# Hybrid decoder layer, one core: the state-space input, q and k projections change which operand stands still in TensorE

## The chip, the cores and the metric

The kernel runs on one core of one Trainium2 chip. The metric is the device time of one execution in microseconds (us); lower is better.

## The reference, cut to what matters

```
h    = rmsnorm(x, ln_g)                      # x: 256 tokens x 4096, float32
proj = h @ w_in                              # 4096 x 12288
p_x, p_gate, q, k, v, a_gate, s_u, s_gate = split(proj)    # 1024 1024 2048 2048 2048 2048 1024 1024
y_pool = pool_mixer(p_x); y_attn = stick_breaking_attention(q, k, v)   # 16 heads of 128
y_ssm  = s5_mixer(s_u)                       # scan over tokens, GELU, GLU with w_glu 1024 x 2048
y = concat(rmsnorm(y_i, g_i) * silu(gate_i)) # pool, attention, state space
out = rmsnorm(x + y @ w_out, final_g)        # w_out 4096 x 4096
```

All is float32. On TensorE each float32 operand is split into a rounded part `hi` and a remainder `lo` (both of the type fp32r), and a product is three matmuls: hi·hi, hi·lo and lo·hi.

## The kernel before, in words

**The stream.** The weights come in 528 pieces of 512 KB (two blocks of 128 rows x 512 columns; "sub" below), in an order that is written out in `IN_ORDER` (L40). 512 columns of one weight make a **unit**: 16 subs for a unit of `w_in` or `w_out`, 4 for one of `w_glu`. The order is su, su (state-space input), px, px, pg, pg, sg, sg, then v, q, k three times, four units of `w_glu`, v, q, k once more, four of ag, and eight of `w_out`. The loop at L860 takes one sub after the other: it issues the loads (SP queue, four subs ahead, L871), splits the weights of the sub two ahead (`split`, L210: ACT rounds `hi` at L228, DVE subtracts `lo` at L231, which the profile shows as its helper L82), and issues the matmuls of this sub into the unit's PSUM tile `pm` (two buffers of 128 x 2 x 512). At the end of a unit `finish` (L766) evacuates the tile. Generators then carry the branches' own work: `pump(side_q, 3)` (L916) takes three steps per sub from the queue of pooling, gates and attention, L917 to L921 take steps of the state-space scan. The framework's scheduler orders the instructions of each engine from a simulated time line and from their dependencies; only SP's order is by hand.

**Two kinds of units.** The normalised and split input `xhl` lies with channels on the partitions: for each of 32 channel blocks, hi and lo of 256 tokens.

- `mm_tok` (L234; px, pg, sg, v, glu, ag, out): 128 tokens stand in the array, 512 weight columns move. A sub is 12 matmuls of 512 columns, a unit of 16 subs is 192. The product has tokens on the partitions; `scaled` (L657) evacuates it with two ACT instructions that multiply by the norm's factor `rtok`, one number per partition.
- `mm_chan` (L241; su, q, k): 128 weight columns stand, 256 tokens move. A sub is 24 matmuls of 256 columns, a unit is 384. The product has channels on the partitions, which is what the scan and the attention's scores want; `chan_scaled` (L663) evacuates it with two DVE instructions that multiply by `rrow`, the norm's factors along the free axis. `norm_x` (L269) makes `rrow` from `rtok` with two matmuls against the identity (L277) and a copy (L278).

There are 10 units of the second kind: 2 su, 4 q, 4 k. The first su unit's product waits in its PSUM tile until the norm is known, at sub 12 of the second unit (L866). 64 PE transposes against the identity exist elsewhere: `transposed` (L291, L296) turns the gated branch outputs, four blocks of 128 x 128 into one PSUM tile `ps_t`, evacuated by ACT. The pool of PSUM tiles tagged `ps` has two buffers and serves these, the scan (`ps_bu`, `ps_y`) and attention (`ps_av`).

**Waits around the change.** `uT` (the turned su product) is read by DMAs that the ACT queue issues (L531, `side_dma`) and by DVE (L577). The tiles `qt` and `kt` are read by the score matmuls of attention (L598, L599), which run in the next unit.

Of the kernel before, what the change touches and what calls it, by code (L numbers as in the profile page):

```python
# [19 lines left out]
P = 128  # L20
# [35 lines left out]
def body(tc, a, out, ctx):  # L56
# [41 lines left out]
    oneneg = cp.tile([P, P], F32R, name="oneneg")  # L98
    identb = cp.tile([P, P], BF16, name="identb")
    maskb = cp.tile([P, P], BF16, name="maskb")  # L100
    ones = cp.tile([P, P], F32, name="ones")
    prm = cp.tile([P, 72], F32, name="prm")
    rtok = cp.tile([P, 2], F32, name="rtok")
    rrow = cp.tile([P, L], F32, name="rrow")
    ln_g = prm[:, 0:32]
    branch_g = prm[:, 32:64]
    d_skip = prm[:, 64:72]
# [10 lines left out]
        stt(t, t, -0.5, dst, ALU.mult, ALU.mult)  # L118
        stt(dst, t, 1.5, dst, ALU.add, ALU.mult)

# [1 line left out]
    wtiles, htiles = {}, {}  # L122
    held = []

# [113 lines left out]
            T.matmul(ps[t], stat[:, slot, 0, sl], lo, start=False, stop=False)  # L238
            T.matmul(ps[t], stat[:, slot, 1, sl], hi, start=False, stop=last)  # L239

    def mm_chan(ps, slot, hi, lo, first, last):  # L241
        for j in range(4):
            o = ps[:, j // 2, (j % 2) * L:(j % 2) * L + L]
            c = slice(j * P, j * P + P)
            T.matmul(o, hi[:, c], xhl[:, slot, 0, :], start=first and j % 2 == 0, stop=False, skip_group_check=True)  # L245
            T.matmul(o, hi[:, c], xhl[:, slot, 1, :], start=False, stop=False, skip_group_check=True)  # L246
            T.matmul(o, lo[:, c], xhl[:, slot, 0, :], start=False, stop=last, skip_group_check=True)  # L247

# [1 line left out]
    state = {}  # L250
    xtiles = {}
    x_sums = cp.tile([P, 2, 8], F32, name="x_sums")
# [16 lines left out]
    def norm_x():  # L269
        s = cp.tile([P, 2], F32, name="s_x", tag="s_b", bufs=2)  # L270
        V.tensor_reduce(s, x_sums, mybir.AxisListType.X, ALU.add)
        rsqrt_mean(rtok, s, 2, D, cp, "rs")
        ps2 = pk.tile([P, 512], F32, tag="ps", bufs=2, name="ps_r")
        for t in range(2):
            rb = cp.tile([P, P], F32, tag="rb", bufs=1, name="rb")
            ts(rb, ones, rtok[:, t:t + 1], ALU.mult)
            T.matmul(ps2[:, t * P:t * P + P], rb, ident, start=t == 0, stop=True, skip_group_check=True)  # L277
        V.tensor_copy(rrow, ps2[:, 0:L])  # L278

# [1 line left out]
    def log1pexp_parts(z, l):  # L281
        act(l, z, AF.Abs)
        act(l, l, AF.Exp, scale=-1.0)
# [43 lines left out]
        if g2 is not None:  # L327
            tt(y, y, g2, ALU.mult)

# [1 line left out]
    pool_sums = cp.tile([P, 2, 2], F32, name="pool_sums")  # L331
    ypool = {}

# [39 lines left out]
        y = ypool.pop(u)  # L373
        yield from transposed(y, [4 * u + c for c in range(4)], keep(lambda kt: ypT[:, kt, :]))

# [1 line left out]
    uT = bp.tile([P, 8, L], F32, tag="k8", bufs=3, name="uT")  # L377
    glu = {}

# [202 lines left out]
            tt(uT[:, ct, :], y, l, ALU.mult)  # L582
            yield

# [1 line left out]
    aout = {}  # L586
    att_sums = cp.tile([P, 2, 4], F32, name="att_sums")

# [62 lines left out]
        else:  # L651
            yield from transposed(y, kts, direct)

# [1 line left out]
    cur = {}  # L655

    def scaled(ps, name):  # L657
# [2 lines left out]
            act(z[:, t, :], ps[:, t, :], AF.Copy, scale=rtok[:, t:t + 1])  # L660
        return z

    def chan_scaled(dst, ps, scale=None):  # L663
        row = rrow.unsqueeze(1).broadcast_to([P, 2, L])
        for h in range(2):
            src = ps[:, h, :].rearrange("p (c m) -> p c m", c=2)
            if scale is None:
                tt(dst[:, 2 * h:2 * h + 2, :], src, row, ALU.mult)
            else:
                stt(dst[:, 2 * h:2 * h + 2, :], src, scale, row, ALU.mult, ALU.mult)  # L670

    ssm_q, side_q = deque(), deque()

# [11 lines left out]
    def drain(q):  # L685
        pump(q, 1 << 30)

# [1 line left out]
    units = []  # L689
    for kind, c in IN_ORDER:  # L690
        units.append((kind, c, 8 if kind == "glu" else KT))
# [24 lines left out]

    def constants():
        nc.sync.dma_start(ident, a["cst"][0])
        V.memset(ones, 1.0)
        for i, dst in ((1, tneg), (2, oneneg), (3, maskb)):  # L720
            raw = cp.tile([P, P], F32, name="raw", tag="rb", bufs=1)
            nc.sync.dma_start(raw, a["cst"][i])
            act(dst, raw, AF.Copy)
        V.tensor_copy(identb, ident)
# [41 lines left out]
    def finish(kind, c, n, ps):  # L766
        nonlocal sgate
        if kind == "su":
            if n == 0:
                state["ps0"] = ps  # L770
                return
            chan_scaled(uT[:, 4:8, :], ps)
            u_done[0] = 8
        elif kind == "px":
            side_q.append(pool_unit(n, scaled(ps, "px")))
        elif kind == "pg":
            side_q.append(pool_gate(n, scaled(ps, "pgz")))
        elif kind == "sg":
            if n == 0:
                sgate = bp.tile([P, 2, 2 * NU], F32, tag="k8", bufs=3, name="sgate")  # L780
            z = scaled(ps, "sgz")

            def sgate_gen(z=z, n=n):
                sg = bp.tile([P, 2, NU], F32, tag="k4", bufs=6, name="sgm")
                sigmoid_of(z, sg)
                yield
                tt(sgate[:, :, n * NU:n * NU + NU], z, sg, ALU.mult)
                yield
            side_q.append(sgate_gen())
        elif kind == "v":  # L790
            cur["v"] = scaled(ps, "vt")
        elif kind in ("q", "k"):
            t = bp.tile([P, 4, L], F32, tag="k4", bufs=6, name=kind + "t")
            chan_scaled(t, ps, QS if kind == "q" else None)
            cur[kind] = t
            if kind == "k":
                if apool is None:
                    start_att()
                if n == 2:
                    start_late()  # L800
                side_q.append(attention(apool if n < 2 else lp, n, cur["v"], cur["q"], cur["k"]))
        elif kind == "glu":
            bias = lp.tile([P, NU], F32, tag="bias", bufs=1, name="bias")
            side_dma(bias, a["bgl"][n:n + 1, :].partition_broadcast(P))
            y = bp.tile([P, 2, NU], F32, tag="k4", bufs=6, name="gl")
            tt(y, ps, bias.unsqueeze(1).broadcast_to([P, 2, NU]), ALU.add)
            if n % 2 == 0:
                def gate_gen(y=y):
                    sg = bp.tile([P, 2, NU], F32, tag="k4", bufs=6, name="gs")
                    glu["sg"] = sg  # L810
                    sigmoid_of(y, sg)
                    yield
                side_q.append(gate_gen())
            else:
                def val_gen(y=y, n=n):
                    tt(y, y, glu.pop("sg"), ALU.mult)
                    yield
                    square_sums(glu_sums, y, n // 2)
                    yield
                    glu[n // 2] = y  # L820
                    if n == 3:
                        r = branch_norm(glu_sums, 1024)
                        ysT = bp.tile([P, 8, L], F32, tag="k8", bufs=3, name="ysT")
                        state["ysT"] = ysT
                        for u in range(2):
                            yu = glu.pop(u)
                            gated(yu, r, sgate[:, :, u * NU:u * NU + NU])
                            yield
                            yield from transposed(yu, [24 + 4 * u + c for c in range(4)], keep(lambda kt: ysT[:, kt - 24, :]))
                side_q.append(val_gen())  # L830
        elif kind == "ag":
            z = scaled(ps, "agz")
            if n == 2:
                drain(side_q)
                att_ctx.close()
                qp = ctx.enter_context(tc.tile_pool(name="rows", bufs=1, reuse_waits="tile"))
                side_q.append(sums_of_rows(qp, y_src))
            side_q.append(att_gate(lp, n, z))
            if n == 3:
                for i in range(28):  # L840
                    hi_lo(xhl[:, i, 0, :], xhl[:, i, 1, :], y_src(i))
        elif kind == "out":
            xr, fg = state["rest"]
            o = state["o"][:, :, n * NU:n * NU + NU]
            tt(o, ps, xr, ALU.add)
            for t in range(2):
                act(xr[:, t, :], o[:, t, :], AF.Square, accum_out=out_sums[:, t, n:n + 1])
            tt(o, o, fg.unsqueeze(1).broadcast_to([P, 2, NU]), ALU.mult)
# [11 lines left out]
    for i, (ui, s) in enumerate(subs):  # L860
# [5 lines left out]
        if ui == 1 and s == 12:  # L866
            with tc.high_priority():
                norm_x()
                chan_scaled(uT[:, 0:4, :], state.pop("ps0"))
            u_done[0] = 4  # L870
        while loaded < min(len(subs), i + 1 + LOAD_AHEAD):  # L871
            if loaded == 0:
                load_first()
# [23 lines left out]
        else:  # L897
            for kk in range(2):
                hi, lo = htiles.pop((i, kk))
                slot = 2 * s + kk  # L900
                first, last = slot == 0, slot == nk - 1
                if kind in ("su", "q", "k"):
                    mm_chan(ps, slot, hi, lo, first, last)
                else:
                    late = i >= N_SUB - HELD
                    mm_tok(psl, hhl if kind == "glu" else xhl, slot, hi, lo, first, last, (0,) if late else (0, 1))
                    if late:
                        delayed.append((slot, hi, lo, last))
        if s == nk // 2 - 1:
            n = nth.get(kind, 0)  # L910
            nth[kind] = n + 1
# [129 lines left out]
```

## Time and profile before

| | us |
|---|---|
| median of 3 runs | 1558.77 (1558.5 to 1559.57) |
| profiled execution, first to last instruction | 1556.4 |
| TensorE busy in it | 1538.2 |

The page of the profile gives the profiled execution's span; what lies around the span is taken as the 2.4 us by which the median stands above it. PE stands for TensorE's matmuls and PEld for its weight loads, DVE for VectorE, ACT for ScalarE, SP for SyncE. A matmul's own duration overlaps with its neighbours', so the cost of one in a dense stretch is the distance between starts.

### The profile page before, as it was taken

The page shows a single profiled execution, that of the slowest core. Times are in us where ns is not written, and L with a number is a line of the kernel's source. Part 1 is how long each engine was busy: PE and PEld are TensorE (multiplying, and loading weights), DVE is VectorE, ACT ScalarE, POOL GpSimd, SP SyncE. Part 2 cuts the span into 40 slices and gives each one's busy share as a digit, 9 for nine tenths or more (in the row PEclk, how much of TensorE's full clock was granted, in tenths as well). Part 3 has the DMA queues.
Part 4 walks back from the last instruction along what each step waited for, and adds up shares of the span by engine and source line. Part 5 has one row for each costly group of instructions (what it writes and reads, how often), then busy time and mean ns, then how long its engine had stood idle before and what let it go on. Part 6 is the DMA issues. An engine that isn't in the chain of part 4 may idle for free.

```text
span 1556.4 us, 25428 instructions
## 1 busy us (share of the span) xinstructions
PE 1538.2 (99%) x9164; PEld 1360.9 (87%) x9164; DVE 1201.6 (77%) x2325; ACT 913.9 (59%) x1637; POOL 0.2 (0%) x4
## 2 busy tenths in 40 slices
PE   8999999999999999999999999999999999999996
PEld 8998788888799989998998889988888888888885
DVE  7579978999898879897556745455678888888886
ACT  7655556666565555565546754456667655555554
POOL 0000000000000000000000000000000000000000
PEclk9999999999999999999999999999999999999999
DMA  8866656566655546554555555545556666666665
GB/s 320 306 214 205 195 162 205 186 206 194 205 188 185 187 156 197 176 175 162 183 186 180 180 185 183 183 159 186 190 178 193 212 220 220 216 214 210 204 222 198
DMA packets 94079, 308.45 MB, mean 198 GB/s; under 512 B 11777, under 2 KB 17665, under 8 KB 93953
## 3 DMA queue, kind: packets, MB, share of 16 engines
q1 hardware_dynamic: 84096, 296.08, 58.2%
q10 hardware_dynamic: 9856, 10.76, 2.3%
q8 instruction: 71, 1.16, 0.3%
q14 instruction: 56, 0.45, 0.1%
HBM read 299.45 MB, written 4.19 MB: 195 GB/s over the span
## 4 chain that ended last, share of the span: by engine, by line
PE 96%; DVE 2%; DMA 1%; ACT 1%; issue 0%; SPq 0%; DVEq 0%; ACTq 0%
PE pm L238 18%; PE pm L237 18%; PE pm L239 18%; PE pm L245 10%; PE pm L247 10%; PE pm L246 10%; PE ps L185 3%; PE pm L185 3%; DVE lo L82 1%; PE ps_y L572 1%; DMA w<-in_ws 1%; PE ps_bu L545 0%; ACT hi L228 0%; PE ps_z L598 0%; PE ps_p L356 0%; PE ps_t L296 0%
## 5 line engine op out<-in xcount | busy, mean ns | idle before, releaser
L82 DVE TENSOR_TENSOR lo<-w,hi 128x512 fp32r<-128x512 f32 (+1 forms) x1048 | 696.9, 678 | 273.1 <-ACT hi L228 266.0
L228 ACT ACTIVATE hi<-w 128x512 fp32r<-128x512 f32 x968 | 604.6, 629 | 503.2 <-PE pm L239 204.4
L238 PE MATMUL pm<-lo,xhl 128*128 128x512 f32 x1232 | 482.4, 392 | 0.0
L239 PE MATMUL pm<-hi,xhl 128*128 128x512 f32 x1232 | 480.8, 390 | 0.0
L237 PE MATMUL pm<-hi,xhl 128*128 128x512 f32 x1232 | 480.6, 390 | 0.0
L245 PE MATMUL pm<-xhl,hi 128*128 128x256 f32 x1280 | 363.8, 284 | 5.3 <-ACT xhl L94 5.3
L246 PE MATMUL pm<-xhl,hi 128*128 128x256 f32 x1280 | 363.5, 284 | 0.0
L247 PE MATMUL pm<-xhl,lo 128*128 128x256 f32 x1280 | 363.4, 284 | 0.0
L238 PEld LDWEIGHTS pm<-lo,xhl 128*128 128x128 f32 x1232 | 231.5, 188 | 48.9 <-issue 2.1
L239 PEld LDWEIGHTS pm<-hi,xhl 128*128 128x128 f32 x1232 | 231.4, 188 | 47.3 <-issue 1.2
L237 PEld LDWEIGHTS pm<-hi,xhl 128*128 128x128 f32 x1232 | 231.5, 188 | 46.9 <-issue 0.4
L245 PEld LDWEIGHTS pm<-xhl,hi 128*128 128x128 f32 x1280 | 246.6, 193 | 7.1 <-ACT xhl L94 5.3
L247 PEld LDWEIGHTS pm<-xhl,lo 128*128 128x128 f32 x1280 | 246.6, 193 | 1.2 <-issue 0.8
L246 PEld LDWEIGHTS pm<-xhl,hi 128*128 128x128 f32 x1280 | 246.6, 193 | 0.8 <-issue 0.4
L91 DVE SCALAR_TENSOR_TENSOR et<-et,pw,tr 128x16 f32<-128x16 f32 (+3 forms) x256 | 55.6, 275 | 2.3 <-ACT tr L94 1.9
L94 ACT ACTIVATE sums<-t 128x1024 fp32r<-128x1024 f32 x40 | 42.3, 1058 | 23.8 <-DVE t L82 23.3
L82 DVE TENSOR_TENSOR sums<-t,sums 128x1024 fp32r<-128x1024 f32 x40 | 48.9, 1223 | 8.8 <-ACT sums L94 8.7
L94 ACT ACTIVATE hi<-w 128x256 fp32r<-128x256 f32 x80 | 40.0, 518 | 22.4 <-PE pm L239 18.9
L185 PE MATMUL ps<-sums,s 128*128 128x256 f32 x240 | 46.5, 283 | 1.1 <-DVE sums L82 1.1
L94 ACT ACTIVATE tr<-et,pw 128x32 f32<-128x32 f32 (+3 forms) x128 | 44.7, 384 | 4.7 <-DVE et L91 2.0
L82 DVE TENSOR_TENSOR t<-w 128x512 f32<-128x512 f32 x40 | 27.6, 690 | 24.3 <-DMA w<-in_ws 24.0
L560 DVE TENSOR_TENSOR_SCAN tb<-rho,ta 128x256 f32<-128x256 f32 x64 | 40.6, 676 | 0.1
(258 smaller groups left out, 1261.3 us busy)
## 6 DMA issues: line engine op xcount, KB each, us to landing
w<-in_ws SPq DMA_DIRECT2D x527, 512.0 KB, 3.5
xsq<-in_xr SPq DMA_DIRECT2D x8, 512.0 KB, 7.2
xr<-in_xr SPq DMA_DIRECT2D x8, 512.0 KB, 4.5
out<-o SPq DMA_DIRECT2D x8, 512.0 KB, 4.0
xt<-in_xT SPq DMA_DIRECT2D x15, 256.0 KB, 6.1
b<-in_bst ACTq DMA_DIRECT2D x16, 192.0 KB, 3.6
u<-uT ACTq DMA_DIRECT2D x96, 32.0 KB, 3.0
fg<-in_fg SPq DMA_DIRECT2D x8, 256.0 KB, 5.9
```

Source lines behind the costliest of these rows:

```text
L82: V.tensor_tensor(o, x, y, op)
L91: V.scalar_tensor_tensor(o, x, s, y, op0, op1)
L94: S.activation(o, x, f, **kw)
L185: T.matmul(o, stat[:, p, :], mov[q], start=begin and k == 0, stop=end and k == 2, skip_group_check=True)
L228: made = S.activation(hi, w[:, kk, :], AF.Copy)
L237: T.matmul(ps[t], stat[:, slot, 0, sl], hi, start=first, stop=False)
L238: T.matmul(ps[t], stat[:, slot, 0, sl], lo, start=False, stop=False)
L239: T.matmul(ps[t], stat[:, slot, 1, sl], hi, start=False, stop=last)
L245: T.matmul(o, hi[:, c], xhl[:, slot, 0, :], start=first and j % 2 == 0, stop=False, skip_group_check=True)
L246: T.matmul(o, hi[:, c], xhl[:, slot, 1, :], start=False, stop=False, skip_group_check=True)
L247: T.matmul(o, lo[:, c], xhl[:, slot, 0, :], start=False, stop=last, skip_group_check=True)
L560: V.tensor_tensor_scan(tb[:, c, :], rho[:, pr:pr + 1].broadcast_to([P, L]), ta[:, c, :], 0.0, ALU.mult, ALU.add)
```

## The change

`mm_chan` and `chan_scaled` go; su, q and k units run through `mm_tok` and are evacuated by `scaled`, and a new generator `channels` turns the result with eight PE transposes in two groups of four, each evacuated by ACT into the tile that DVE wrote before. `rrow`, `ones` and the matmuls that made `rrow` go as well.

```diff
-    ones = cp.tile([P, P], F32, name="ones")
-    rrow = cp.tile([P, L], F32, name="rrow")
...
-    def mm_chan(ps, slot, hi, lo, first, last):
-        for j in range(4):
-            o = ps[:, j // 2, (j % 2) * L:(j % 2) * L + L]
-            c = slice(j * P, j * P + P)
-            T.matmul(o, hi[:, c], xhl[:, slot, 0, :], start=first and j % 2 == 0, stop=False, skip_group_check=True)
-            T.matmul(o, hi[:, c], xhl[:, slot, 1, :], start=False, stop=False, skip_group_check=True)
-            T.matmul(o, lo[:, c], xhl[:, slot, 0, :], start=False, stop=last, skip_group_check=True)
...
         rsqrt_mean(rtok, s, 2, D, cp, "rs")
-        ps2 = pk.tile([P, 512], F32, tag="ps", bufs=2, name="ps_r")
-        for t in range(2):
-            rb = cp.tile([P, P], F32, tag="rb", bufs=1, name="rb")
-            ts(rb, ones, rtok[:, t:t + 1], ALU.mult)
-            T.matmul(ps2[:, t * P:t * P + P], rb, ident, start=t == 0, stop=True, skip_group_check=True)
-        V.tensor_copy(rrow, ps2[:, 0:L])
...
-    def chan_scaled(dst, ps, scale=None):
-        row = rrow.unsqueeze(1).broadcast_to([P, 2, L])
+    def channels(z, dst, scale=1.0):
         for h in range(2):
-            src = ps[:, h, :].rearrange("p (c m) -> p c m", c=2)
-            if scale is None:
-                tt(dst[:, 2 * h:2 * h + 2, :], src, row, ALU.mult)
-            else:
-                stt(dst[:, 2 * h:2 * h + 2, :], src, scale, row, ALU.mult, ALU.mult)
+            ps = pk.tile([P, 512], F32, tag="ps", bufs=2, name="ps_c")
+            for c in range(2):
+                for t in range(2):
+                    T.transpose(ps[:, (c * 2 + t) * P:(c * 2 + t + 1) * P], z[:, t, (h * 2 + c) * P:(h * 2 + c + 1) * P], ident)
+            act(dst[:, 2 * h:2 * h + 2, :], ps.rearrange("p (c m) -> p c m", c=2), AF.Copy, scale=scale)
+            yield
+
+    def take_u(ps, n):
+        def gen(z=scaled(ps, "suz")):
+            yield from channels(z, uT[:, 4 * n:4 * n + 4, :])
+            u_done[0] = 4 * n + 4
+        side_q.append(gen())
...
-            chan_scaled(uT[:, 4:8, :], ps)
-            u_done[0] = 8
+            take_u(ps, 1)
...
             t = bp.tile([P, 4, L], F32, tag="k4", bufs=6, name=kind + "t")
-            chan_scaled(t, ps, QS if kind == "q" else None)
+            side_q.append(channels(scaled(ps, kind + "z"), t, QS if kind == "q" else 1.0))
...
                 norm_x()
-                chan_scaled(uT[:, 0:4, :], state.pop("ps0"))
-            u_done[0] = 4
+                take_u(state.pop("ps0"), 0)
...
-                if kind in ("su", "q", "k"):
-                    mm_chan(ps, slot, hi, lo, first, last)
-                else:
-                    late = i >= N_SUB - HELD
-                    mm_tok(psl, hhl if kind == "glu" else xhl, slot, hi, lo, first, last, (0,) if late else (0, 1))
+                late = i >= N_SUB - HELD
+                mm_tok(psl, hhl if kind == "glu" else xhl, slot, hi, lo, first, last, (0,) if late else (0, 1))
```

## Rows read from the trace of the kernel before

**Rows 1.** The page: busy time and instructions of each engine.
```profile
PE 1538.2 (99%) x9164; PEld 1360.9 (87%) x9164; DVE 1201.6 (77%) x2325; ACT 913.9 (59%) x1637; POOL 0.2 (0%) x4
```

**Rows 2.** The page: the chain that ended last, by line.
```profile
PE pm L238 18%; PE pm L237 18%; PE pm L239 18%; PE pm L245 10%; PE pm L247 10%; PE pm L246 10%; PE ps L185 3%; PE pm L185 3%; DVE lo L82 1%; PE ps_y L572 1%; DMA w<-in_ws 1%; PE ps_bu L545 0%; ACT hi L228 0%; PE ps_z L598 0%; PE ps_p L356 0%; PE ps_t L296 0%
```

**Rows 3.** Waits, whole span: who waited for whom, us, times, longest.
```profile
ACT hi L228 <- PE pm L239: 204.4, 273, 2.7
ACT hi L228 <- PE pm L246: 190.2, 258, 1.6
PE pm L245 <- ACT xhl L94: 5.3, 1, 5.3
```

**Rows 4.** PE timeline at both ends of the last k unit.
```profile
969.39 0.28 PE L245 MATMUL pm<-xhl,hi 128*128 128x256 f32 x1
...
1015.47 0.40 PE L237 MATMUL pm<-hi,xhl 128*128 128x512 f32 x1
```

**Rows 5.** Busy time by stretch, one unit each: su, su, sg, q, k, ag.
```profile
core 0: us, PE busy (x) PEld busy (x) DVE busy (x) ACT busy (x) POOL busy (x), PEclk, DMA share, GB/s
5.27:53.94 48.67, 48.67 (x385) 48.44 (x386) 36.63 (x69) 34.92 (x68) 0.00 (x0) 1.00 0.88 311
53.94:100.44 46.50, 46.50 (x390) 46.50 (x389) 25.50 (x50) 30.87 (x68) 0.00 (x0) 1.00 0.80 289
295.58:341.54 45.96, 45.96 (x211) 37.61 (x210) 45.13 (x92) 30.42 (x54) 0.00 (x0) 1.00 0.63 197
434.73:482.02 47.29, 47.29 (x397) 46.74 (x395) 44.86 (x98) 27.06 (x51) 0.00 (x0) 1.00 0.60 192
969.39:1015.47 46.08, 46.08 (x386) 46.08 (x385) 23.36 (x34) 20.20 (x32) 0.00 (x0) 1.00 0.55 183
1066.81:1111.23 44.42, 44.42 (x202) 36.88 (x200) 25.43 (x37) 26.28 (x42) 0.00 (x0) 1.00 0.58 190
```

**Rows 6.** PE timeline of the eight transposes in that ag unit.
```profile
1080.41 0.39 PE L237 MATMUL pm<-hi,xhl 128*128 128x512 f32 x1
1080.65 1.03 PE L296 MATMUL ps_t<-ident,ao 128*128 128x128 f32 x8
1081.44 0.48 PE L238 MATMUL pm<-lo,xhl 128*128 128x512 f32 x1
1081.75 0.40 PE L239 MATMUL pm<-hi,xhl 128*128 128x512 f32 x1
```

**Rows 7.** Busy time by stretch, the first 10 us of matmuls.
```profile
5.27:10.44 5.17, 5.17 (x23) 4.94 (x23) 3.39 (x7) 3.55 (x8) 0.00 (x0) 1.00 1.01 342
10.44:15.00 4.56, 4.56 (x39) 4.56 (x39) 4.36 (x9) 4.12 (x9) 0.00 (x0) 1.00 1.03 407
```

**Rows 8.** Instructions on tiles vt, qt, kt, ps_t: ns min/median/max, first and last start.
```profile
L94 ACT ACTIVATE vt<-pm,rtok x8: 677/684/690, 434.9 to 924.1; 128x512 f32<-128x512 f32 x8
L91 DVE SCALAR_TENSOR_TENSOR qt<-pm,rrow x8: 681/686/693, 482.1 to 970.2; 128x512 f32<-128x512 f32 x8
L82 DVE TENSOR_TENSOR kt<-pm,rrow x8: 677/680/692, 530.4 to 1016.3; 128x512 f32<-128x512 f32 x8
L296 PE MATMUL ps_t<-ident,ao x32: 270/272/274, 1080.6 to 1215.8; 128*128 128x128 f32 x32
```

**Rows 9.** ACT timeline just after a v unit ended at 434.73.
```profile
434.93 1.26 ACT L94 ACTIVATE vt<-pm,rtok 128x512 f32<-128x512 f32 x2 [0.20 <-PE pm L239]
436.08 0.63 ACT L228 ACTIVATE hi<-w 128x512 fp32r<-128x512 f32 x1
```

**Rows 10.** DVE, then PE timeline after the first k unit (ended at 529.81).
```profile
530.44 1.28 DVE L82 TENSOR_TENSOR kt<-pm,rrow 128x512 f32<-128x512 f32 x2
...
535.27 0.39 PE L237 MATMUL pm<-hi,xhl 128*128 128x512 f32 x1
535.50 0.59 PE L598 MATMUL ps_z<-qt,kt 128*128 128x256 f32 x2
```

**Rows 11.** Tiles rtok and ao: norm's factor, last attention sum.
```profile
L91 DVE SCALAR_TENSOR_TENSOR rtok<-rs_t,rtok x1: 152/152/152, 89.8 to 89.8; 128x2 f32<-128x2 f32 x1
L94 ACT ACTIVATE junk<-ao x8: 613/623/632, 577.4 to 1062.2; 128x512 bf16<-128x512 f32 x8
```

More of the change, by code (lines that the diff above doesn't have):

```diff
@@ L718, in constants @@
         nc.sync.dma_start(ident, a["cst"][0])
-        V.memset(ones, 1.0)
         for i, dst in ((1, tneg), (2, oneneg), (3, maskb)):
@@ L901, in body @@
                 first, last = slot == 0, slot == nk - 1
-                if kind in ("su", "q", "k"):
-                    mm_chan(ps, slot, hi, lo, first, last)
-                else:
-                    late = i >= N_SUB - HELD
-                    mm_tok(psl, hhl if kind == "glu" else xhl, slot, hi, lo, first, last, (0,) if late else (0, 1))
-                    if late:
-                        delayed.append((slot, hi, lo, last))
+                late = i >= N_SUB - HELD
+                mm_tok(psl, hhl if kind == "glu" else xhl, slot, hi, lo, first, last, (0,) if late else (0, 1))
+                if late:
+                    delayed.append((slot, hi, lo, last))
         if s == nk // 2 - 1:
```

## The prediction

> **What bounds the kernel now.** First the page's busy times: PE is busy for 99% of the span, DVE for 77%, ACT for 59% [rows 1]. PE's busy time alone proves little, because its ends are modelled, so the second view is the chain that ended last: 84% of it are the six lines of `mm_tok` and `mm_chan`, and 30% are L245 to L247, the ones to be replaced [rows 2]. The third view is the waits. ACT's rounding of weights mostly waits for PE to give back a buffer (204.4 and 190.2 us), while the list's largest wait of PE is the one at the very start, 5.3 us [rows 3]. The suppliers are ahead and PE sets the pace. So what counts is the time of a unit on PE, and the stretches say it unit by unit: in every one PE is busy from end to end, whatever else runs [rows 5].
>
> **The main matmuls.** The last k unit starts at 969.39 and the next unit at 1015.47 [rows 4]: 46.08 us with nothing else in it, so 46.08 / 384 = 0.120 us for a matmul of 256 columns. An ag unit is, on PE, what a changed unit will be: 192 matmuls of 512 columns and eight transposes. It takes 44.42 us [rows 5]. From the first of its transposes to the second matmul behind them are 1.10 us (1080.65 to 1081.75); one matmul of some 0.227 is in that, so the eight cost 0.87 [rows 6], and (44.42 - 0.87) / 192 = 0.227 us for 512 columns. Twice 0.120 is 0.240: each matmul carries about 13 ns beside its columns, and the change halves their number. A unit saves 46.08 - 44.42 = 1.66 us: 2.53 from the matmuls, 0.87 given back to the transposes. Ten units: 16.6 us.
>
> How the transposes are priced matters. One lasts 272 ns by its own duration [rows 8], but the eight hold the next matmul up by 0.87 us together, 0.11 each. I take the second, since it is the path's. The Trainium skill (TensorE: Matmul & The Clock Gate, Part 4) gives about 275 ns for a 128 x 128 transpose inside a kernel; as path time that would be an estimate of 22 us for eighty instead of 8.7, and a total near 1555. The trace agrees with the figure as a latency and disagrees with it as a cost.
>
> **Two corrections.** The second su unit takes 46.50, 0.42 more than the bare 46.08 [rows 4, 5]; it holds the four matmul instructions of `rrow`, which go: 0.4 us gained. At the start 23 matmuls take 5.17 us, against 39 in the next 4.56 [rows 7]; the granted clock reads 1.00 in both, so the row doesn't say why, and I assume that in this slow stretch time goes by columns and nothing is saved: 23 x (0.120 - 0.113) = 0.15 us lost. The bounds of that term are 0 and 0.2.
>
> **What lies beside.** DVE loses two instructions of 0.68 us per unit, ACT gains two like `vt`'s, 0.68 each, and two evacuations from PSUM of the same 128 x 512, for which I take the same 0.68 [rows 8]; bounds are nothing and all 2.7 us of a unit. I cost them at nothing: in the k unit ACT is busy for 20.20 of 46.08 us, in the fullest of the listed q units for 27.06 of 47.29 [rows 5], and behind them on ACT stands the rounding of the next sub, which waits for PE's buffers anyway [rows 3]. If that cover were gone, at most 2.7 us a unit would show. The DMAs that read `uT` are issued from ACT's queue and come behind the new instructions; they feed the scan, which PE doesn't wait for as long as its steps are placed by readiness. SP's and POOL's queues get nothing new. The scores of attention read `kt`, ready by 531.72 (530.44 + 1.28) and used at 535.50 [rows 10]. Now it takes ACT's two, the transposes and ACT's two: 0.2 + 1.3 + 0.9 + 1.4, some 4 us after the unit's end at 529.81 plus queueing, so the scores slide by 0 to 3 us. The last attention sum is started at 1062.2, before the ag unit's end at 1066.81 [rows 5, 11], where its norm is first wanted. For the first su unit `rtok` is there at 89.8, and its PSUM tile is wanted at 100.44 [rows 5, 11]; both move forward by 3 to 5 us together. The `ps` pool gets 20 more tiles over ten units; I cost them at nothing because each is freed by one ACT instruction.
>
> **The sum.** 16.6 + 0.4 - 0.15 = 16.85 us. The profiled span goes from 1556.4 to 1539.5; with the 2.4 us around it, the median from 1558.77 to **1541.9**.
>
> **Rivals.**
>
> *The suppliers become the bound.* Beside the scan DVE is nearly full: 45.13 of 45.96 us in an sg unit, 44.86 of 47.29 in the first q unit [rows 5]. After the change the q unit has 44.86 - 1.37 = 43.5 us of DVE in 45.6, 95% as now, and the sg unit shows that PE runs unbroken at 98%; that speaks against. The two su units are fed at 311 and 289 GB/s and would need some 5% more; 342 and 407 were reached in the first stretches [rows 5, 7]. If four q and k units beside the scan kept their time, 4 x 1.66 = 6.6 are lost: 1548.5; with both su units as well 9.9: 1551.8.
>
> *PE waits in front of the transposes* (the case on the slower side). The generator is pumped in the same sub as the unit's end. If the transposes stand right behind the last matmul, PE, which goes in order, waits for `scaled`: a v unit ended at 434.73 and its two scalings at 436.19, 1.46 us later [rows 9], or 2.1 if a rounding of 0.63 comes between. Behind PE's wait stands the whole next unit. Ten times that is 15 to 21 us: 1556.5 to 1563. It decides from 1.69 us a unit on; there the change is a loss. Against it: the scheduler puts dependent work where it expects it ready. The scores of attention come 5.7 us after the unit's end, between the next unit's matmuls and without a gap [rows 10], and the present transposes stand inside a unit in the same way [rows 6].
>
> *A matmul costs its columns and next to nothing more*, so that the change doesn't remove what it seems to. Then the new units take 46.08 again plus 0.87: 8.7 us more, less 0.4, 1567. The Trainium skill has this rule (TensorE: Matmul & The Clock Gate, Part 1, the paragraph on 56 ns): at the full clock, columns at 2.4 GHz plus about 2.5 ns. By it the estimate is 1920 x 2.5 ns = 4.8 us saved, less than the transposes take, and about 1562. The trace disagrees: 0.120 and 0.227 us stand some 13 ns above 256 and 512 columns at 2.4 GHz. Without the page the rows alone decide it: the units already of the new form, ag here, run at 0.227 a matmul, in the same code.
>
> **How the numbers follow.** The forecast as summed has 0.70; the suppliers 0.15; waits before the transposes 0.10, of which a third would still be faster because only some units are struck; columns alone 0.02; 0.03 for what I don't see. This kernel's measurement can tell 0.2%, 3.1 us, from no change: faster means under 1555.7. Faster 0.70 + 0.15 + 0.03 = 0.88; within 0.2% 0.05; slower 0.07. The range goes down to 1538, which allows for rounding in the unit times and for somewhat better placement, and up to 1552, which takes in the suppliers' case whole.
>
> **What the profile would show.** Right: 7320 PE matmul instructions (9164 - 3840 + 1920 + 80 - 4); a k unit of the last group at 44.4 us with matmuls 0.227 apart, no gap around eight transposes; DVE about 1.4 us shorter and ACT about 2.7 us longer a unit. Wrong: idle PE at the start of the units behind su, q and k, released by ACT (waits); q and k units beside the scan longer than 45.6 us with PE waiting for `lo` (suppliers); 0.240 between matmuls (columns). If the units are short and the total isn't, the time must come back in the units of gates or output, and the stretches there would be longer than before.

## The result, and the profile after

The changed kernel takes 1539.30 us (median of 4 runs, 1538.63 to 1540.72) against 1559.17 for the kernel before beside it: 0.9875 of its time, 95% interval 0.9861 to 0.9889. The forecast was 1541.9, 16.85 us less; measured are 19.9 in the medians and 19.5 in the profiled spans (1556.4 to 1536.9). The direction and most of the size came as forecast; some 2.7 us of the spans' difference were not in the sum.

The page of the changed kernel, busy time and chain, answers to [rows 1, 2]:

```profile
span 1536.9 us, 21598 instructions
...
PE 1519.2 (99%) x7320; PEld 1266.7 (82%) x7320; DVE 1185.8 (77%) x2301; ACT 933.0 (61%) x1677; POOL 0.2 (0%) x4
...
PE pm L236 29%; PE pm L235 29%; PE pm L237 29%; PE ps L183 4%; PE pm L183 3%; PE ps_y L556 1%; PE ps_c L652 1%; PE ps_bu L529 1%; PE ps_t L280 0%; PE ps_z L582 0%; PE ps_p L340 0%; PE ps_z L600 0%; PE ps_av L612 0%; PE ps_av L613 0%; DMA xt<-in_xT 0%; PE ps_av L611 0%
```

PE has the 7320 instructions that were counted out, and it still sets the end. ACT has 40 instructions more, DVE 24 fewer. `mm_tok` is now L235 to L237, the new transposes L652. The same units as in [rows 5], by stretch (su, su, sg, q, and the last k):

```profile
core 0: us, PE busy (x) PEld busy (x) DVE busy (x) ACT busy (x) POOL busy (x), PEclk, DMA share, GB/s
5.85:52.18 46.33, 46.33 (x193) 38.11 (x193) 36.23 (x69) 34.37 (x68) 0.00 (x0) 1.00 0.91 323
52.18:96.60 44.42, 44.42 (x202) 36.83 (x200) 23.58 (x52) 32.04 (x72) 0.00 (x0) 1.00 0.83 302
291.79:337.75 45.96, 45.96 (x212) 37.61 (x211) 45.12 (x92) 30.39 (x54) 0.00 (x0) 1.00 0.62 197
430.93:475.08 44.15, 44.15 (x198) 36.65 (x197) 42.82 (x95) 26.45 (x50) 0.00 (x0) 1.00 0.63 202
...
951.61:996.02 44.41, 44.41 (x201) 36.86 (x200) 22.10 (x33) 22.24 (x36) 0.00 (x0) 1.00 0.56 189
```

The last k unit takes 44.41 us where it took 46.08, and the sg unit is unchanged to the hundredth. PE's timeline of the changed kernel, the transposes of that k unit in the unit behind it (`ps_c`), answers to [rows 6, 10]:

```profile
996.02 0.39 PE L235 MATMUL pm<-hi,xhl 128*128 128x512 f32 x1
...
1001.01 0.39 PE L236 MATMUL pm<-lo,xhl 128*128 128x512 f32 x1
1001.24 1.03 PE L652 MATMUL ps_c<-ident,kz 128*128 128x128 f32 x8
1002.03 0.48 PE L237 MATMUL pm<-hi,xhl 128*128 128x512 f32 x1
1002.35 0.40 PE L235 MATMUL pm<-hi,xhl 128*128 128x512 f32 x1
```

The k unit ends at 996.02, and PE does 5.2 us of the next unit's matmuls before it turns the result. There is no gap, and the distances are those of [rows 6]: 1.11 us from the first transpose to the second matmul behind, one matmul in it.

**Where the time went.** Both spans cut at the same unit boundaries, from the start of su to the end: su to the first pg; pg to v; q, k, v; q, k, v; q, k and the four `w_glu` units; v, q, k and the first ag; the other ag units; the output stage. First the kernel before:

```profile
5.27:248.69 243.42, 243.42 (x1443) 216.13 (x1443) 196.48 (x499) 148.43 (x294) 0.00 (x0) 1.00 0.70 234
248.69:434.73 186.04, 186.04 (x855) 149.55 (x853) 169.60 (x349) 122.13 (x222) 0.00 (x0) 1.00 0.62 196
434.73:582.36 147.63, 147.63 (x1052) 137.59 (x1051) 126.01 (x260) 83.73 (x153) 0.00 (x0) 1.00 0.55 179
582.36:733.00 150.64, 150.64 (x1066) 138.75 (x1065) 132.98 (x281) 86.05 (x160) 0.00 (x0) 1.00 0.55 179
733.00:877.98 144.98, 144.98 (x1027) 135.83 (x1026) 85.23 (x129) 81.61 (x136) 0.00 (x0) 1.00 0.56 179
877.98:1066.81 188.83, 188.83 (x1225) 173.08 (x1224) 101.71 (x156) 95.30 (x162) 0.00 (x0) 1.00 0.56 181
1066.81:1200.06 133.25, 133.25 (x601) 110.63 (x600) 93.83 (x164) 89.21 (x159) 0.00 (x0) 1.00 0.58 187
1200.06:1556.40 356.34, 343.43 (x1905) 299.35 (x1903) 294.77 (x490) 205.05 (x351) 0.00 (x0) 0.99 0.65 213
```

The changed kernel, the same stretches:

```profile
5.85:244.89 239.04, 239.04 (x1070) 197.02 (x1071) 191.79 (x490) 151.12 (x302) 0.00 (x0) 1.00 0.69 237
244.89:430.93 186.04, 186.04 (x854) 149.53 (x853) 170.15 (x351) 122.11 (x222) 0.00 (x0) 1.00 0.60 196
430.93:573.99 143.06, 143.06 (x679) 118.82 (x677) 120.27 (x251) 86.64 (x158) 0.00 (x0) 1.00 0.58 187
573.99:720.21 146.22, 146.22 (x697) 119.49 (x696) 128.27 (x275) 90.65 (x171) 0.00 (x0) 1.00 0.55 182
720.21:862.65 142.44, 142.44 (x666) 117.26 (x665) 87.32 (x132) 84.38 (x140) 0.00 (x0) 1.00 0.56 185
862.65:1048.23 185.58, 185.58 (x859) 154.72 (x858) 97.66 (x146) 100.06 (x171) 0.00 (x0) 1.00 0.54 181
1048.23:1181.48 133.25, 133.25 (x602) 110.59 (x600) 94.87 (x170) 90.87 (x165) 0.00 (x0) 1.00 0.56 188
1181.48:1536.90 355.42, 343.55 (x1905) 299.26 (x1903) 294.60 (x490) 204.79 (x349) 0.00 (x0) 0.99 0.64 213
```

| stretch | measured | forecast | the rest |
|---|---|---|---|
| su, su to the first pg | -4.38 | -3.6 | -0.8 |
| q, k, v | -4.57 | -3.3 | -1.2 |
| q, k, v | -4.42 | -3.3 | -1.1 |
| q, k, glu | -2.54 | -3.3 | +0.8 |
| v, q, k, ag | -3.25 | -3.3 | +0.1 |
| output stage | -0.92 | 0 | -0.9 |
| start of the first matmul | +0.58 | 0 | +0.6 |

Two stretches hold no su, q or k unit and come before the output stage (pg to v, and the later ag units); they differ by 0.00. The output stage's -0.9 is one wait for sums of split weights, which PE's list of waits shows in the kernel before alone:

```profile
PE ps L185 <- DVE sums L82: 1.1, 1, 1.1
```

The reversed kernel before (first experiment) doesn't have that wait either, so it is not put down to the change. Nor is the start: the first matmul comes between 4.7 and 5.9 us in the nine traces, in no order that follows the edits.

What is left of the rest is in four of the five stretches in which the state-space scan runs, and it has both signs. The scan's own PE work there is the same, but PE does it in other pieces. Instructions of `ps_y` alone, over the whole scan, first in the kernel before, then in the changed one:

```profile
160.00:830.00 670.00, 17.14 (x128) 5.01 (x128) 3.84 (x8) 1.00 0.58 185
```

```profile
160.00:830.00 670.00, 14.69 (x128) 4.50 (x128) 3.84 (x8) 1.00 0.57 188
```

The same 128 records keep PE busy for 17.14 us before and 14.69 after. PE's timeline of the kernel before shows why that can be (the matmul before, the visit, the first matmul behind):

```profile
179.72 0.39 PE L237 MATMUL pm<-hi,xhl 128*128 128x512 f32 x1
180.04 0.62 PE L572 MATMUL ps_y<-s,cf 128*32 128x256 f32 x2
180.59 0.50 PE L238 MATMUL pm<-lo,xhl 128*128 128x512 f32 x1
...
197.93 0.39 PE L238 MATMUL pm<-lo,xhl 128*128 128x512 f32 x1
198.25 1.05 PE L572 MATMUL ps_y<-s,cf 128*32 128x256 f32 x10
199.23 0.50 PE L239 MATMUL pm<-hi,xhl 128*128 128x512 f32 x1
```

Two records take 0.55 us from their start to the next matmul, ten take 0.98. By the same distances, with the slower steps around a visit added, a visit costs 0.75 us with 2, 4 or 6 records and 1.18 with 10. The kernel before makes 22 visits (20.0 us), the changed one 18 (17.0 us). By stretch, for the first four rows of the table, that is -0.7, -1.5, -1.5 and +0.8, which is the rest within 0.4 in each; from pg to v both kernels make the same eight visits. It seems that the scheduler places a `ps_y` matmul as soon as it expects its state to be ready, and that with shorter units the pieces fell otherwise. This was a reading of two traces; the first two experiments test it.

### The profile page after: what moved, and what is told of

Read it like the earlier page. It is cut to its first block, busy times and chain, and to the rows that moved or that the text cites. A ratio compares the mean times of both kernels' runs of the same rounds, so it can differ in the third digit from the quotient of the medians.

```text
span 1536.9 us, 21598 instructions
## 1 busy us (share of the span) xinstructions
PE 1519.2 (99%) x7320; PEld 1266.7 (82%) x7320; DVE 1185.8 (77%) x2301; ACT 933.0 (61%) x1677; POOL 0.2 (0%) x4
## 4 chain that ended last, share of the span: by engine, by line
PE 99%; DVE 0%; DMA 0%; ACT 0%; SPq 0%; DVEq 0%; issue 0%; ACTq 0%
PE pm L236 29%; PE pm L235 29%; PE pm L237 29%; PE ps L183 4%; PE pm L183 3%; PE ps_y L556 1%; PE ps_c L652 1%; PE ps_bu L529 1%; PE ps_t L280 0%; PE ps_z L582 0%; PE ps_p L340 0%; PE ps_z L600 0%; PE ps_av L612 0%; PE ps_av L613 0%; DMA xt<-in_xT 0%; PE ps_av L611 0%
## 5 line engine op out<-in xcount | busy, mean ns | idle before, releaser
L235 PE MATMUL pm<-hi,xhl 128*128 128x512 f32 x1872 | 731.4, 391 | 5.9 <-ACT xhl L94 5.9
L236 PE MATMUL pm<-lo,xhl 128*128 128x512 f32 x1872 | 732.9, 392 | 0.0
L237 PE MATMUL pm<-hi,xhl 128*128 128x512 f32 x1872 | 731.3, 391 | 0.0
L235 PEld LDWEIGHTS pm<-hi,xhl 128*128 128x128 f32 x1872 | 352.3, 188 | 79.1 <-ACT xhl L94 5.9
L236 PEld LDWEIGHTS pm<-lo,xhl 128*128 128x128 f32 x1872 | 352.4, 188 | 74.2 <-issue 2.9
L237 PEld LDWEIGHTS pm<-hi,xhl 128*128 128x128 f32 x1872 | 352.1, 188 | 71.4 <-issue 0.8
L183 PEld LDWEIGHTS ps<-sums,s 128*128 128x128 f32 x240 | 36.7, 192 | 0.4 <-DVE sums L82 0.2
L82 DVE TENSOR_TENSOR t<-w,t 128x256 f32<-128x256 f32 x80 | 33.5, 419 | 0.3
L94 ACT ACTIVATE sgm<-sgm 128x1024 f32<-128x1024 f32 x24 | 25.2, 1051 | 0.2
L237 PE MATMUL pm<-hi,hhl 128*128 128x512 f32 x64 | 25.2, 394 | 0.0
L236 PE MATMUL pm<-lo,hhl 128*128 128x512 f32 x64 | 25.2, 393 | 0.0
L235 PE MATMUL pm<-hi,hhl 128*128 128x512 f32 x64 | 25.1, 392 | 0.0
```

The lines of the kernel that those rows point to most:

```text
L82: V.tensor_tensor(o, x, y, op)
L94: S.activation(o, x, f, **kw)
L183: T.matmul(o, stat[:, p, :], mov[q], start=begin and k == 0, stop=end and k == 2, skip_group_check=True)
L235: T.matmul(ps[t], stat[:, slot, 0, sl], hi, start=first, stop=False)
```

## The experiments

The kernel before was run again beside the experiments: its median was 1559.17 us beside the changed kernel, 1557.84 beside the first four experiments and 1558.60 beside the last three. A difference between kernels of different sessions is uncertain by about that much, 1 us.

**One visit to ps_y, in both kernels.** Each channel tile's `ps_y` is eight matmuls, four states by real and imaginary part. In reverse order the last state comes first, so that none of the others is issued ahead of it. The same edit in the kernel before and in the changed one:

```diff
-            for c in range(2):
-                for j in range(4):
-                    T.matmul(ps[32 * j:32 * j + 32, 0:L], cf[:, j, c, :], ss[j][:, c, :], start=c == 0, stop=c == 1, skip_group_check=True)
+            for c in (1, 0):
+                for j in (3, 2, 1, 0):
+                    T.matmul(ps[32 * j:32 * j + 32, 0:L], cf[:, j, c, :], ss[j][:, c, :], start=c == 1, stop=c == 0, skip_group_check=True)
```

Expected of the kernel before with it:

> The kernel before, with the eight ps_y matmuls of a channel tile in reverse order, so that the one that waits longest comes first. In the trace before, PE visits ps_y 22 times between other matmuls, and a visit costs 0.75 us whether it holds 2, 4 or 6 matmul records and 1.18 with 10: 20.0 us in all. Theory (a visit has a price of its own): 8 visits at about 1.2 us, 9.6 us, so 10 us less than before, about 1549. Rival (the price is that of the work, or PE then waits for the last state): within 2 us of before, or slower.

Expected of the changed kernel with it:

> The changed kernel with the same reversal. It has 18 visits to ps_y at 17.0 us instead of 22 at 20.0; that difference of 2.9 us is my candidate for the part of the gain that the sum did not have. Theory: about 1539.3 - 7.4 = 1532, and the difference to the reversed kernel before is the sum of the forecast, 16.9 us, with no rest. Rival (the rest comes from something else, such as shorter waits in the output stage alone): the difference stays at 19 us or more.

Measured: 1546.82 us for the reversed kernel before (0.9930 of the kernel before, 0.9917 to 0.9942) and 1530.82 for the reversed changed kernel (0.9826, 0.9813 to 0.9840), against 1557.84 for the kernel before in the same session. That is 11.0 us less where 10 were expected, and 1531 where 1532 was. One visit in the reversed kernel before, on PE's timeline, and then `ps_y` over its whole scan:

```profile
197.73 1.07 PE L572 MATMUL ps_y<-s,cf 128*32 128x256 f32 x16
198.73 0.50 PE L237 MATMUL pm<-hi,xhl 128*128 128x512 f32 x1
```

```profile
160.00:830.00 670.00, 8.57 (x128) 3.34 (x128) 3.81 (x8) 1.00 0.56 187
```

All 16 records of a tile take 1.00 us to the next matmul, hardly more than ten did, and the 128 records keep PE busy for half the time. In the reversed changed kernel the sum is the same, 8.56. With the visits equal the two kernels differ by 16.0 us in the medians, where the forecast's sum is 16.85 and the unequal pair differs by 19.9: most of the rest that the sum lacked was the visits. It came with the change but is not what the change does. The reversal by itself is worth 11.0 us in the kernel before and 7 to 8.5 in the changed one, which has fewer visits to lose. The reversed changed kernel is also the fastest version here.

The profiled spans of the reversed pair, 1545.0 and 1530.3, differ by 14.7 only. From the first matmul to the end of the last ag unit they differ by 16.1 (1185.0 and 1168.9 us); the output stage of the changed one is 1.4 longer in that execution, the slowest of its four, by waits that the last section shows. So the sum of the forecast is some 0.7 us too large where nothing else differs.

**Half the columns.** In su, q and k each matmul of 512 columns becomes two of 256; the operand that stands, the evacuation and the transposes are those of the changed kernel.

```diff
+    def mm_half(ps, slot, hi, lo, first, last):
+        for t in range(2):
+            sl = slice(t * P, t * P + P)
+            for n in range(2):
+                c = slice(n * L, n * L + L)
+                T.matmul(ps[t][:, c], xhl[:, slot, 0, sl], hi[:, c], start=first and n == 0, stop=False, skip_group_check=True)
+                T.matmul(ps[t][:, c], xhl[:, slot, 0, sl], lo[:, c], start=False, stop=False, skip_group_check=True)
+                T.matmul(ps[t][:, c], xhl[:, slot, 1, sl], hi[:, c], start=False, stop=last, skip_group_check=True)
...
+                if kind in ("su", "q", "k"):
+                    mm_half(psl, slot, hi, lo, first, last)
+                    continue
```

> The changed kernel, but in su, q and k each matmul of 512 moving columns is issued as two of 256; tokens still stand, and the transposes stay. Theory (about 13 ns beside the columns for each matmul, whichever operand stands): 10 x 2.53 = 25 us more than the changed kernel, about 1564.5, slower than before by the transposes. Rival (the gain comes from tokens as the stationary operand, their loads or their ports, not from the count): about 1539.

Measured: 1564.48 us, 1.0046 of the kernel before (1.0032 to 1.0060), 25 us above the changed kernel (26.5 when each is held against the kernel before of its own session). It makes 20 visits to `ps_y` instead of 18, some 1.4 us of that. Its last k unit, which holds the eight transposes of the q unit before it, as one stretch:

```profile
974.96:1021.91 46.95, 46.95 (x394) 46.95 (x393) 22.08 (x33) 22.28 (x36) 0.00 (x0) 1.00 0.53 180
```

46.95 - 0.87 = 46.08, the time of the old k unit [rows 4], with the other operand standing; and 46.95 against 44.41 in the changed kernel are 13 ns for each of the 192 matmuls more. So the whole gain on the matmuls is their number, and which operand stands is worth nothing by itself. Every matmul has one weight load here (x394 and x393 in the row), so matmuls and loads were halved together, and the 13 ns can belong to either. The rival of the stationary operand falls, and with it the rule that a matmul costs its columns and next to nothing more.

**The transposes forced in front.** PE's order is fixed so that the transposes of a unit precede the next unit's first matmul, without a wait added.

```diff
-            T.matmul(ps[t], stat[:, slot, 0, sl], hi, start=first, stop=False)
+            m = T.matmul(ps[t], stat[:, slot, 0, sl], hi, start=first, stop=False)
+            if first and t == 0 and "turned" in state:
+                tc.add_manual_dep(
+                    m.ins, state.pop("turned"),
+                    mybir.DependencyInfo(mybir.DependencyClass.NoSync, mybir.DependencyReason.DATA),
+                    reason="behind the transposes",
+                )
...
-                    T.transpose(ps[:, (c * 2 + t) * P:(c * 2 + t + 1) * P], z[:, t, (h * 2 + c) * P:(h * 2 + c + 1) * P], ident)
+                    state["turned"] = T.transpose(ps[:, (c * 2 + t) * P:(c * 2 + t + 1) * P], z[:, t, (h * 2 + c) * P:(h * 2 + c + 1) * P], ident).ins.name
```

> The changed kernel with PE's order fixed so that the eight transposes of a unit come before the first matmul of the next unit (for nine of the ten units; the first su unit's stay inside the second). Theory (what was forecast as the slower rival): PE waits 1.5 to 2.1 us for the two scalings in each, 13 to 19 us in all, 1553 to 1558, which gives back most of the gain. Rival (the scalings come soon enough, or the wait is made up later): under 1545.

Measured: 1553.75 us, 0.9972 of the kernel before (0.9961 to 0.9983), 14.5 above the changed kernel (15.8 by the kernels before of the two sessions). PE's waits in it, and PE's timeline at the end of the last k unit:

```profile
PE ps_c L658 <- ACT kz L94: 3.1, 4, 0.8
PE ps_c L658 <- ACT qz L94: 2.3, 3, 0.8
PE ps_c L658 <- DVE tb L82: 1.5, 1, 1.5
PE ps_c L658 <- ACT suz L94: 0.9, 1, 0.9
...
PE ps_c L658 <- ACT qt L94: 0.7, 1, 0.7
```

```profile
1008.14 0.39 PE L243 MATMUL pm<-hi,xhl 128*128 128x512 f32 x1
1009.31 1.46 PE L658 MATMUL ps_c<-ident,kz 128*128 128x128 f32 x8 [0.78 <-ACT kz L94]
1010.52 0.47 PE L235 MATMUL pm<-hi,xhl 128*128 128x512 f32 x1
```

From the unit's last matmul to the next unit's first are 2.38 us, of which 0.23 are that matmul's and 0.87 and a little more the transposes': some 1.3 are the wait for the two scalings. The row's 0.78 is less, because a matmul's modelled end lies after the next could have started. Eight of the nine units show this distance, 2.38 to 2.49 us; the ninth, a q unit, takes 3.65, with waits of 1.5 and 0.7 us that end with a DVE and an ACT instruction, probably for `ps` buffers. Together that is nearly all of the 13.3 us by which the span grew. So the slower rival's mechanism is real, and its price of 1.5 to 2.1 us a unit was right at its lower end; the changed kernel escapes it by its order alone.

**The parts alone.** Both on the reversed kernel before, so that the visits stay equal: the change for su only, and for q and k only. The edit is the diff of the change, undone for q and k in the first, as shown, and for su in the second; what is undone has `mm_chan`, `chan_scaled` and `rrow` again.

```diff
+                if kind in ('q', 'k'):
+                    mm_chan(ps, slot, hi, lo, first, last)
+                    continue
```

> The reversed kernel before (one visit to ps_y per channel tile) with the change for the two su units alone; q and k stay as before, with rrow. Theory: two units at 1.66 us less, and nothing from rrow: 1546.8 - 3.2 = 1543.6. Rival (the first units are held by their loads and the norm, so that su gains nothing): 1546.8.

> The reversed kernel before with the change for the eight q and k units alone; su stays as before, with rrow. Theory: 8 x 1.66 = 13.3 us less: 1546.8 - 13.3 = 1533.5, and together with the su units the 16 us between the two reversed kernels. Rival (the units beside the scan are held by DVE or ACT): only the last four q and k units gain, 6.6 us, 1540.

Measured: su alone 1543.38 us (0.9903 of the kernel before at 1558.60, 0.9888 to 0.9918), q and k alone 1534.44 (0.9842, 0.9826 to 0.9859). Against the reversed kernel before, at 1546.82 in the other session, that is 3.4 and 12.4 us, 15.8 together, where the whole change gave 16.0 and 3.2 and 13.3 were expected; allowing for the 0.8 us between the sessions it is 4.2 and 13.1. Either way the su units are not held by their loads, nor the q and k units beside the scan by DVE or ACT: with the gain of the last four q and k units alone 1540 would have been measured.

**The transposes twice.** Each of the 80 is issued twice into the same place, in the reversed changed kernel.

```diff
-                    T.transpose(ps[:, (c * 2 + t) * P:(c * 2 + t + 1) * P], z[:, t, (h * 2 + c) * P:(h * 2 + c + 1) * P], ident)
+                    for again in range(2):
+                        T.transpose(ps[:, (c * 2 + t) * P:(c * 2 + t + 1) * P], z[:, t, (h * 2 + c) * P:(h * 2 + c + 1) * P], ident)
```

> The reversed changed kernel with each of the 80 transposes issued twice into the same place. Theory (0.11 us each on PE's path): 80 x 0.109 = 8.7 us more than the reversed changed kernel, 1530.8 + 8.7 = 1539.5. Rival 1 (each costs its own duration of 0.27 us): 1552. Rival 2 (transposes hide between other matmuls): 1531.

Measured: 1539.41 us (0.9876, 0.9861 to 0.9891), 8.6 more than the reversed changed kernel for 80 transposes, 7.8 when each is held against its own session's kernel before: 0.10 to 0.11 us each. PE's timeline of one group:

```profile
1000.79 1.91 PE L653 MATMUL ps_c<-ident,kz 128*128 128x128 f32 x16
1002.45 0.48 PE L237 MATMUL pm<-hi,xhl 128*128 128x512 f32 x1
```

Sixteen take 1.66 us to the next matmul where eight took 0.79: 0.11 us for each one more.

## Why the prediction was right, step by step

**The bound.** Right: PE set the pace before and sets it after, and the sg unit and the two stretches without an edited unit kept their time to the hundredth.

**The main matmuls.** Right. A changed unit takes what the ag unit took, 44.42 and 44.41 us against 46.08. The half-column kernel showed the reason to be the count: 2.54 us a unit for 192 matmuls more, 13 ns each. Reading the price of a new unit from an old one of the same form left little to estimate.

**The transposes.** Right at 0.11 us each on PE's path, in the trace and by doubling them. Their own duration, here again 270 to 273 ns, is a latency. The Trainium skill's figure of about 275 ns for a 128 x 128 bf16 transpose inside a kernel (TensorE: Matmul & The Clock Gate, Part 4) agrees with the duration of these float32 ones. As a cost it gives an estimate of 22 us for the second eighty, and about 8 were measured.

**The corrections.** The transposes of the first su unit stand in the second, and those of the second in the first px unit. The first lost 48.67 - 46.33 = 2.34 us, close to the forecast's 2.53 for the matmuls less its 0.15 for the slow start; the second lost 46.50 - 44.42 = 2.08, which is 1.66 + 0.42; the px unit grew from 44.04 to 44.92. The three together came within 0.1 us of the sum. The assumption about the slow start was right: the first matmuls of 512 columns come 0.427 us apart in the changed kernel, twice the 0.213 of 256 columns before.

**What lies beside.** Right that it costs nothing, with one price too high. These are the changed kernel's instructions that evacuate the turned tiles:

```profile
L94 ACT ACTIVATE qt<-ps_c x8: 581/596/601, 481.5 to 958.1; 128x512 f32<-128x512 f32 x8
L94 ACT ACTIVATE kt<-ps_c x8: 580/596/601, 527.5 to 1002.5; 128x512 f32<-128x512 f32 x8
L94 ACT ACTIVATE uT<-ps_c x4: 594/599/601, 93.1 to 103.4; 128x512 f32<-128x512 f32 x4
```

They take 0.60 us, not `vt`'s 0.68, and ACT is busy for 1.9 us a unit more (933.0 - 913.9 over ten), not 2.7. `kt` was complete some 7 us after a unit's end, in one unit 12.4, not 4, because the transposes were placed late. The scores, which begin 10.6 to 11.6 us after a k unit's end, slid by 5 to 6 us, not 0 to 3, and PE's list of waits shows none for them. DVE is busy for 42.82 of 44.15 us in the first q unit, 97%, and PE still doesn't wait.

**The sum.** 16.85 us were too few by 2.7 in the spans. The term that was missing is the cost of the work that was not edited: the sum took the scan's instructions on PE at an unchanged price. Their order was the scheduler's, and moved with the units' lengths. The visits to `ps_y` gave 2.9 us and the output stage 0.9; the later first matmul took 0.6, and some 0.5 of the sum didn't come. The range held the result because its lower end allowed for better placement, though the text gave no mechanism for it: for the 2.7 us that was luck, for the 16.85 it was not.

**The rivals.** The suppliers did not become the bound. The wait before the transposes is real and would have cost about 15 us; its own forecast of 15 to 21 was near, but even so the kernel would have stayed faster than before by 0.3%: nine units waited and not ten, at the low end of the price, and with 19 visits to `ps_y` some of the visits' gain lay under it. Columns alone is refuted by the half-column kernel. The Trainium skill's rule for it (TensorE: Matmul & The Clock Gate, Part 1, the paragraph on 56 ns), measured there on back-to-back bf16 matmuls, is about 2.5 ns beside the columns and doesn't hold for these: 13 ns were read from the trace and measured by splitting. What makes up the 13 ns was not tried.

## What to carry to other kernels

Where PE is the bound, price a new form of a unit by an existing unit of that form in the same trace, and price a short instruction by the distance it opens between its neighbours, not by its duration. A transpose that undoes a better matmul shape is cheap if the scheduler can put it a few microseconds behind its producer; directly behind, it gives most of the gain back. Before crediting an edit with its whole gain, see whether PE's other work came in the same pieces: small matmuls that trickle out as their inputs come ready can be held together by issuing the last-ready one first, and that alone gave 11 us in the kernel before.

## What was not expected of the hardware

A visit of PE to the `ps_y` matmuls (128 rows by 32 stationary columns, 256 moving, plain float32, four column groups in turn) costs 0.75 us with two records and 1.2 with sixteen. A tile's sixteen records took 1.9 us in two visits and 3.4 in four, in one visit 1.2. One after the other, at the 0.120 us of a 256-column matmul [rows 4], sixteen would take 1.9; so matmuls of different column groups run beside each other when they stand together. The distances suggest rounds: two to six records take 0.55 us to the next matmul, ten to sixteen 0.98 to 1.00, and the step of 0.43 is what one full-width score matmul (`ps_z`, two records, 256 columns) takes. Then a visit costs about 0.33 us and a round 0.43, and the reversal saved some of both, 14 visits and 14 rounds. This is an estimate from the traces; the two were not tested apart.

With the visits joined, PE's list of waits shows a new one, in the reversed changed kernel:

```profile
PE pm L236 <- DVE held L82: 1.1, 1, 1.1
...
PE pm L235 <- ACT held L226: 0.3, 1, 0.3
```

Some 1.4 us of waiting for split weights (`held`) appear in the last output unit, in the execution that was profiled. The kernel with the change in q and k alone shows 0.7 us for `held`, the one with the transposes doubled none. So the suppliers can be close there; whether a further gain on PE would be lost to them was not tested.
